# Running the DeltaNet chains of two heads step by step beside each other in a hybrid decoder kernel

## The chip, the core and the metric

The kernel runs on one core of one Trainium2 chip, in one launch. The metric is the device time of that launch in microseconds (us), lower is better. The engines in the texts are PE (TensorE, the matrix engine), PEld (its weight loads), DVE (VectorE), ACT (ScalarE), POOL (GpSimd) and SP (SyncE, which here issues the DMAs). `L110` means line 110 of the kernel before.

## The reference

The kernel is one inference step of a trunk of two layers: 2048 prompt tokens with 16 learned meta tokens ahead of them, and 8 sample tokens with caches and states of their own. The width is 1024, all in float32. Layer AB projects its normed input once and feeds two mixers: window attention (8 query heads, 2 key heads, window 128, a learned sink per head) and gated DeltaNet (4 heads of 128, a short causal convolution on q, k and v, and a recurrent state). Both are gated, put side by side and projected back. Layer C is a gated linear attention (GLA) with 4 heads. The DeltaNet of one head, cut to its core:

```python
a_mat = jnp.where(strict, jnp.einsum('bnhik,bnhjk->bnhij', kbeta, kc) * decay, 0.0) + jnp.eye(CHUNK)
rhs = jnp.concatenate([vc * bc[..., None], kbeta * jnp.exp(gc)[..., None]], axis=-1)
sol = lax.linalg.triangular_solve(a_mat, rhs, left_side=True, lower=True, unit_diagonal=True)
u, w = sol[..., :B_DV], sol[..., B_DV:]
...
def step(S, xs):
    u_c, w_c, qk_c, qd_c, kd_c, gl_c = xs
    v_new = u_c - jnp.einsum('bhck,bhkv->bhcv', w_c, S)
    o = jnp.einsum('bhck,bhkv->bhcv', qd_c, S) + jnp.einsum('bhij,bhjv->bhiv', qk_c, v_new)
    S = S * gl_c[..., None, None] + jnp.einsum('bhck,bhcv->bhkv', kd_c, v_new)
    return S, o
```

So each head needs, for every chunk of tokens, the inverse of a unit lower triangular matrix (it is the same for all the right-hand sides), and then a scan over the chunks that carries the state `S`. The heads don't depend on each other.

## The kernel before, in words

**Tiling.** The prompt is worked in four groups of 512 tokens; group 0 carries 24 tokens more (8 sample, 16 meta), and works its columns in two halves of 268. A group goes through layer AB and then layer C. The activations lie transposed (features on partitions, tokens along the free axis).

**Two kinds of products.** The large projections come from `proj`: one output tile of 128 features takes 8 feature blocks of 3 matmuls each (values are split into a high and a low part in a rounded float type, and high x high, high x low and low x high are added up), with 512 columns. They accumulate in the PSUM pool `pp`, 4 buffers. All the small products (DeltaNet, attention, GLA) are plain f32 matmuls and accumulate in the PSUM pool `pc`, also 4 buffers, which `cb` hands out. `MM` is the helper at L110, and `TT`, `STT` and `TS` are those at L113, L116 and L120, so most rows of the profile bear these lines; tiles tell them apart (`wh` and `wl` are the high and the low part of a weight).

**The planner.** The program's order is worked out in Python while the program is built. The projections are the trunk: `bulk` (L406) issues them and adds what three matmuls take to a clock of TensorE, `Clock.pe`. Everything else is a chain: a generator that emits a step and then yields two numbers, the time until its next step is due and what the step cost TensorE. `spawn` (L383) puts a chain into a lane; the chains of one lane run one after another. After every three projection matmuls `bulk` runs those chains whose step is due (`step`, L392). `join` (L418) runs chains until the named ones are done, without any projection between them. `take` and `give` (L434, L442) count work tiles: tag `T` has 52 slots with a cap of 47 (`NT - NT_FREE`), tag `BQ` has 4. Where there is no room, `take` runs the chains until there is; within a chain, `take_in` and `until` look again every 0.5 us of the planner's clock. The times until due are the table `LAT` (`DEF_LAT`, L34). The compiler's scheduler may still move an instruction within its engine's queue by the readiness that it models.

**The DeltaNet chain of a head**, `dn_head` (L1420), on four chunks of 128 tokens, with a yield between the steps:

1. four transposes of k (L1450), its norm on ACT, the decay (`R`), the products of k with k and q, four transposes of the masked product (`at`);
2. the inverse: first on DVE the 32x32 diagonal blocks (`i1`, L1498 to L1505), then four levels of doubling, each of two steps (`ia` and `ib`, L1506 to L1524) of 16 products of 32x32 with a DVE operation and a DVE transpose between them; then two steps of L1530 to L1551 that join blocks of 32 to 64, and two steps (L1554, L1559) of 64x64 products that join those to 128; the temporaries are the tiles `inv`, 6 buffers;
3. transposes of v and q (L1567, L1575), then for each chunk the three steps of the scan (`s1`, `s2`, `s3`, L1582 to L1602), then the norm, a last transpose and the gate.

The due times of a chain add up to 47.84 us. `ab_conv` takes 2 tiles of `T` (`CV` and the gate) and 2 of `BQ` (`CQ` and one that the chain works in) for a head, and its chain 7 more of `T` (2 in `chunks`, 5 in `dn_head`); of the 9, two stay until the output projection as the mixed tile.

**The order around the change.** `ab_conv` (L893) projects and convolves k, q and v of a head (j = 0, 1, 2), and spawns its chain into the lane "dn" at j = 1. In group 0 it also spawns the chains of the meta tokens (`meta`) and of the sample tokens (`dn_sample`), in lanes of their own. `ab_head` (L1044) does head 0; from group 1 on it runs within the previous group's `c_out` (L1303). `ab_rest` (L1050) follows the order

```python
ORDER = "c1 s0 c2 s1 c3 s2 s3".split()
```

where `c` is a DeltaNet head and `s` one of four pairs of attention heads: `ab_swa` (L957) takes 3 tiles, projects, and spawns `swa_pair` (L983), which takes 6 more and works four blocks of 128 queries (due times 21.7 us), in the lane "swa". Then `ab_out` (L1062) gives back the 16 tiles of the layer's input and projects the 8 mixed tiles to the output: a first half from those in `OUT_AB[:3]`, which are heads 0 and 1 and pair 0 (in group 0 heads 0 and 1 only), then a `join` of all DeltaNet and attention chains, then the second half. Layer C follows: `c_head` (L1239), `gla_head` (L1751), `c_out`.

Of the kernel before, what the change touches and what calls it, by code (L numbers as in the profile page):

```python
# [9 lines left out]
F32 = mybir.dt.float32  # L10
# [10 lines left out]
SMP = 8  # L21
META = 16
EX = SMP + META
NT, NT_FREE = 52, 5
NW = 8
AHEAD = 8
W_AHEAD = 1
RS_AT = 5

ORDER = "c1 s0 c2 s1 c3 s2 s3".split()  # L30

# [4 lines left out]
CMAX = EX + 512  # L36
# [33 lines left out]
def kernel(ctx: ExitStack, tc: tile.TileContext, ins, outs):  # L70
# [12 lines left out]
    def nm(s):  # L83
        cnt[0] += 1
        return f"{s}_{cnt[0]}"
# [9 lines left out]
        return ft(dt)  # L95

    def t512(shape=(128, 128), dt=F32):
        return wk.tile(list(shape), dt, tag="t512", bufs=4, name=nm("t5"))

    def sm(shape=(128, 32), dt=F32):  # L100
        return wk.tile(list(shape), dt, tag="sm", bufs=20, name=nm("sm"))

    def cb(shape=(128, 512)):
        return pc.tile(list(shape), F32, tag="pc", name=nm("pc"))
# [278 lines left out]
    def spawn(gen, lane, delay=1.0, tag=None):  # L383
        s = [Clock.pe + delay, gen, True, lane, tag]
        if lanes.setdefault(lane, []):
            lanes[lane].append(s)
        else:
            lanes[lane].append(s)
            streams.append(s)
        return s  # L390

    def step(s):  # L392
        try:
            lat, pe = next(s[1])
            s[0] += lat
            Clock.pe += pe
        except StopIteration:
            s[2] = False
            streams.remove(s)
            lanes[s[3]].pop(0)  # L400
            if lanes[s[3]]:
                n = lanes[s[3]][0]
                n[0] = max(n[0], s[0])
                streams.append(n)

    def bulk(gen, hooks=()):  # L406

        for i, c in enumerate(gen):
# [3 lines left out]
            while streams:  # L412
# [2 lines left out]
                    break  # L415
                step(s)

    def join(ss):  # L418
        while any(s[2] for s in ss):
            advance()  # L420


    live = {"BQ": 0, "T": 0}
    caps = {"BQ": 4, "T": NT - NT_FREE}

    def room(tag, n=1):
        return live[tag] + n <= caps[tag]
# [15 lines left out]
        live[tag] -= n  # L443

    def until(cond):
        while not cond():
            yield 0.5, 0.0

    def take_in(tag, n=1):
        yield from until(lambda: room(tag, n))  # L450
# [213 lines left out]
    def new_group(g):  # L664
        q = Grp()
        q.g = g
        q.C = CMAX if g == 0 else 512
        q.off = EX if g == 0 else 0
        q.halves = [(0, q.C // 2), (q.C // 2, q.C // 2)] if g == 0 else [(0, 512)]
        q.x0 = 0 if g == 0 else EX + 512 * g  # L670
        q.wins = [(b, q.off + 128 * b) for b in range(4)]
        q.seq0 = SMP if g == 0 else 0
        q.s0 = 1 if g == 0 else 0
        q.nscan = 4 + q.s0
        q.layer = "AB"
        q.M = [[None] * 8, [None] * 8]
        q.can_m = False
        q.dn = []
        q.sw = []
        return q  # L680

# [211 lines left out]
    def ab_conv(q, h):  # L893
        g = q.g
        take("BQ", 2)
        CQ = wk.tile([128, 2, CMAX - SMP], F32, tag="BQ", bufs=4, name=nm("CQ"))
        take("T", 2)
        CV = ft(shape=(128, CMAX - SMP))
        G_, vdone, done = [], [], []

        first, got = [], []

        def meta():
            yield from take_in("T")
            got.append(1)
            yield from dn_head(q, h, CQ, CV, 0, 1, 32, 0, G_, SMP, META, vdone, done, first)

        def chunks():
            if g == 0:
                yield from until(lambda: got)  # L910
            else:
                first.append(1)
            yield from take_in("T", 2)
            yield from dn_head(q, h, CQ, CV, META if g == 0 else 0, 4, 128, q.s0, G_, q.off, 128, vdone, done, first)
            give("BQ")
            give("T")
        for j in range(3):
            ct = 3 * h + j
            Tt = ft()

            def w(i):
                return PV[:, P_CW + 4 * ct + i:P_CW + 4 * ct + i + 1]

            def ev_c(ps, c0, n):

                m = n - q.seq0
                if g == 0:
                    A.copy(XS[:, ct, :], ps[:, 0:SMP])
                    R = ps[:, SMP - 3:n]
                    V.memset(R[:, 0:3], 0.0)  # L930
                else:
                    R = ft()
                    A.copy(R[:, 3:3 + m], ps)
                    G.tensor_copy(R[:, 0:3], hist[:, ct])
                A.activation(Tt[:, :m], R[:, 3:3 + m], AF.Copy, scale=w(3))
                for i in (2, 1, 0):
                    STT(Tt[:, :m], R[:, i:i + m], w(i), Tt[:, :m], mul, add)
                G.tensor_copy(hist[:, ct], R[:, m:m + 3])
                o = (CV if j == 2 else CQ[:, j])[:, :m]
                A.activation(o, Tt[:, :m], AF.Tanh, scale=0.5)  # L940
                STT(o, o, 1.0, Tt[:, :m], add, mul)
            bulk(ab_proj(q, 9 + ct, ev_c))
            if h == 0 and j == 0:
                bulk(ab_v(q))
            if j == 1:
                if g == 0:
                    q.dn.append(spawn(meta(), "dnx", 0.5, tag=h))
                s = spawn(chunks(), "dn", LAT["dn_spawn"], tag=h)
                q.dn.append(s)
        vdone.append(1)  # L950
        G_.append(ft())
        bulk(ab_proj(q, 21 + h, gate(q, G_[0], 4 + h)))
        done.append(1)
        if g == 0:
            q.dn.append(spawn(dn_sample(q, h), "smp", tag=h))
# [154 lines left out]
    def c_v(q, h):  # L1110
        g, s0 = q.g, q.s0
        take("BQ")
        VH = wk.tile([128, 4, 256], F32, tag="BQ", bufs=4, name=nm("VH"))
        if h == 0:
            gkp = cb()
            gkx = cb() if g == 0 else None

        def ev_vc(ps, slot):
            ex = slot == "e"
            rsc = q.rs[:, 4:5] if ex else q.rs[:, slot:slot + 1]  # L1120
            if ex:
                e = wk.tile([128, 256], F32, tag="SM", bufs=4, name=nm("exv"))
                A.activation(e[0:EX], ps[0:EX, 0:256], AF.Copy, scale=rsc[0:EX])
                q.VM = wk.tile([128, 256], F32, tag="SM", bufs=4, name=nm("vm"))
                SY.dma_start(q.VM[0:META], e[SMP:EX, :])
                q.VS = e
            else:
                A.activation(VH[:, slot, :], ps[:, 0:256], AF.Copy, scale=rsc)
            if h == 0:
                gt = sm((128, 16))  # L1130
                if ex:
                    TS(gt[0:EX], ps[0:EX, 256:272], rsc[0:EX])
                    T.transpose(gkx[0:16, 0:EX], gt[0:EX], ident[0:EX, 0:EX])
                else:
                    TS(gt, ps[:, 256:272], rsc)
                    T.transpose(gkp[0:16, 128 * slot:128 * slot + 128], gt, ident)
        ws = ([("e", 0, ev_vc)] if g == 0 else []) + [(b, c0, ev_vc) for b, c0 in q.wins]
        if h == 0:
            yield from proj_tok(q, ("cv", h), q.H, 272, ws)
            for (src, c0, n) in [(gkp, q.off, 512)] + ([(gkx, 0, EX)] if g == 0 else []):  # L1140
                V.tensor_copy(GS[0:16, c0:c0 + n], src[0:16, 0:n])
                TT(GS[32:48, c0:c0 + n], src[0:16, 0:n], GS[0:16, c0:c0 + n].bitcast(F32), sub)
                V.tensor_copy(GS[64:80, c0:c0 + n], src[0:16, 0:n])
        else:
            yield from proj_tok(q, ("cv", h), q.H, 256, ws)
        q.VH = VH

    def c_logs(q):
# [3 lines left out]
        yield from take_in("BQ", 2)  # L1152
        q.mn, Bs = [], []
        for p in range(2):
            B = wk.tile([128, 2, CMAX], F32, tag="BQ", bufs=4, name=nm("Bc"))
            for h in (2 * p, 2 * p + 1):
                mn = ft()
                bg = PV[:, P_BGK + h:P_BGK + h + 1]
# [80 lines left out]
    def c_head(q, h, nxt):  # L1239
# [8 lines left out]
        join([q.dec])  # L1248
        E = q.E
        take("BQ", 2)  # L1250
        QKt = wk.tile([128, 2, CMAX], F32, tag="BQ", bufs=4, name=nm("QKt"))
        for j in range(2):
            def ev_m(ps, c0, n):
                TT(QKt[:, j, c0:c0 + n], ps, E[j][:, c0:c0 + n], mul)
# [165 lines left out]
    def dn_head(q, h, CQ, CV, q0, nch, L, s0, G_, mc0, nv, vdone, done, first):  # L1420
# [47 lines left out]
            A.activation(DT[R_, c, 0:L], Rp[R_, c, 0:L], AF.Exp, bias=SC["ng"][R_, s0 + c, h:h + 1])  # L1468
        yield LAT["dn_R"], 0.45 * pe
        if L == 128:  # L1470
            BQ = wk.tile([128, 4, 2, 128], F32, tag="BQ", bufs=4, name=nm("BQ"))
        else:
            BQ = ftt((128, 1, 64)).rearrange("p c (x l) -> p c x l", x=2)
        for c0 in range(0, nch, 2):
# [18 lines left out]


        yield LAT["dn_at"], 0.45 * pe
        tc4 = lambda: wk.tile([128, 4, 32], F32, tag="inv", bufs=6, name=nm("inv"))

        P1, Y, X = tc4(), tc4(), tc4()  # L1498
        for a in range(nb):
# [60 lines left out]
            A.copy(YF[0:64, :, 64:128], pi[0:64, 1])  # L1560
            yield 0.0, 0.4

        while not vdone:
            yield 0.5, 0.0
        vT = cb((128, 4, 128))
        for c in range(nch):
            T.transpose(vT[R_, c], blk(2, c), ident)  # L1567
# [46 lines left out]
        on = O  # L1614
        TT(on[R_, 0:nch], O[R_, 0:nch], bc(st2[R_, 3, 0:nch], 128), mul)
        yield LAT["dn_n"], 0.0
        while not (done and q.can_m):
            yield 0.5, 0.0
        oT = cb((128, 4, 128))
        for c in range(nch):  # L1620
            T.transpose(oT[:, c, 0:L], on[R_, c], ident[R_, 0:L])
# [129 lines left out]
    def gla_head(qq, h, QKt, VH, ce, Gz, done):  # L1751
# [14 lines left out]
        A.copy(KT, kT)  # L1766
        yield LAT["gl_t"], 1.4
        st = sm((128, 4, 4))
        On = wk.tile([128, 4, 256], F32, tag="BQ", bufs=4, name=nm("On"))
        QS = ft(shape=(128, 4, 128))  # L1770
        TT(QS, QKt[:, 0, off:off + 512].rearrange("p (c t) -> p c t", c=4), bc(ce[:, s0:s0 + 4], 128), mul)
        for c0 in (0, 2):
# [31 lines left out]

    def gla_sample(q, h, QKt, VS, ea, Gz):
        vrow = rows_of(VS[0:8], 256)
        QZ = wk.tile([128, 72], F32, tag="t512", bufs=4, name=nm("QZ"))
        V.memset(QZ, 0.0)
        V.tensor_copy(QZ.rearrange("p (b x) -> p x b", x=9)[:, 0, :], QKt[:, 0, 0:SMP])
        o = cb()  # L1810
# [155 lines left out]
```

## Time and profile before

| what | value |
| --- | --- |
| time, median of 3 runs | 2223.04 us (2221.27 to 2227.0) |
| profiled execution, its own time | 2224.94 us |
| span of its trace | 2223.2 us |
| TensorE clock granted, mean | 0.986 of full speed |
| HBM over the span | 179 GB/s |
| DMA packets' time, share of 16 engines | 52.6% (queue of SP) |

The profile is of one execution. Its page lists the busy time of each engine, the chain of work that ended last, and the groups of instructions by line and tile. The busy time of one engine in the groups is a sum over instructions that overlap (matmuls are pipelined), so the distance from the start of one matmul to that of the next is what it costs TensorE's queue, and less than its duration. A row of a group reads: line, engine, operation, output tile <- input tiles, tile shape, number; then busy time and mean duration in ns; then the idle time ahead of these instructions and what ended most of it. A row of the timeline reads: start in us from the span's start, duration, engine, line, operation, tiles, shape, and the number of like instructions in a row; in brackets what it waited for. "x32" in a row of f32 products means 16 products, since an f32 matmul leaves two records.

### The profile page before, as it was taken

The numbers are of one execution on the slowest core, as the hardware profiler recorded it, in microseconds if no ns is written. First come the engines' busy times: TensorE is split into PE (matmuls) and PEld (weight loads), VectorE is DVE, ScalarE is ACT, GpSimd is POOL, SyncE is SP. The second block draws the span as 40 slices with busy tenths as digits, with TensorE's granted clock in tenths as the row PEclk, the third lists the DMA queues.
The fourth block names the chain that finished last, engine by engine and source line by source line (L and its number), as shares of the span: only waits on it lengthen the run. The fifth ranks groups of instructions, "written<-read, shape, count | busy, mean of one in ns | idle before, by whom it ended". The sixth has DMA issues, their size and how long they took to land.

```text
span 2223.2 us, 43787 instructions
## 1 busy us (share of the span) xinstructions
PE 2152.0 (97%) x17290; PEld 1809.8 (81%) x17290; DVE 1231.0 (55%) x3501; ACT 835.4 (38%) x2235; POOL 263.6 (12%) x314
## 2 busy tenths in 40 slices
PE   8889999999999999999999999999999999999997
PEld 8878888888879777788887777788887877778886
DVE  7768876655464566544344466545344466654323
ACT  5435444443352244333332244334333233334222
POOL 0011100021210011002220011002130000001111
PEclk9989999999999999999999999999999999999999
DMA  6643537767766723464555733365554743274444
GB/s 236 211 155 121 175 118 263 253 218 261 253 204 244 242 96 103 135 239 142 181 204 164 267 107 102 125 218 169 180 198 147 245 147 114 86 259 156 157 149 156
DMA packets 162622, 400.17 MB, mean 180 GB/s; under 512 B 22048, under 2 KB 54464, under 8 KB 162384
## 3 DMA queue, kind: packets, MB, share of 16 engines
q1 hardware_dynamic: 162416, 397.37, 52.6%
q8 instruction: 136, 2.23, 0.4%
q14 instruction: 70, 0.57, 0.1%
HBM read 297.19 MB, written 101.70 MB: 179 GB/s over the span
## 4 chain that ended last, share of the span: by engine, by line
PE 69%; DVE 5%; DMA 2%; ACT 2%; issue 2%; POOL 1%; SPq 0%; DVEq 0%; POOLq 0%; ACTq 0%
PE pp L110 53%; PE pc L110 14%; DVE t L116 2%; DVE t L113 1%; DVE inv L113 1%; PE pc L1015 1%; DMA t<-in_xT 1%; PE pc L1796 1%; DMA t<-x2d 1%; POOL sm L206 0%; DVE t L120 0%; DVE t L999 0%; PE pc L1575 0%; PE pc L1450 0%; DMA t<-rows 0%
## 5 line engine op out<-in xcount | busy, mean ns | idle before, releaser
L110 PE MATMUL pp<-t,wh 128*128 128x512 f32 (+1 forms) x4528 | 1265.8, 364 | 17.7 <-DVE t L113 7.7
L110 PEld LDWEIGHTS pp<-t,wh 128*128 128x128 f32 x4528 | 782.6, 191 | 128.4 <-issue 19.6
L110 PE MATMUL pp<-t,wl 128*128 128x512 f32 (+1 forms) x2264 | 808.8, 358 | 1.9 <-DVE wl L113 1.7
L110 PEld LDWEIGHTS pp<-t,wl 128*128 128x128 f32 x2264 | 429.8, 190 | 60.5 <-DVE wl L113 2.7
L113 POOL TENSOR_TENSOR t<-t,t 128x512 fp32r<-128x512 f32 (+3 forms) x128 | 163.8, 1298 | 517.3 <-ACT t L660 275.1
L110 PE MATMUL pp<-wh,t 128*128 128x256 f32 (+1 forms) x1088 | 209.0, 288 | 3.8 <-DVE QKt L113 3.8
L116 DVE SCALAR_TENSOR_TENSOR t<-t,PV,t 128x512 f32<-128x512 f32 (+4 forms) x232 | 176.0, 768 | 60.0 <-ACT t L1098 24.3
L110 PEld LDWEIGHTS pp<-wh,t 128*128 128x128 f32 x1088 | 172.4, 190 | 6.0 <-DVE QKt L113 4.0
L206 POOL TENSOR_TENSOR sm<-sm,mh 128x2 f32<-128x2 f32 (+3 forms) x84 | 68.4, 814 | 812.3 <-DVE sm L116 367.5
L116 DVE SCALAR_TENSOR_TENSOR t<-pp,t 128x512 f32<-128x512 f32 (+3 forms) x160 | 93.1, 586 | 120.0 <-PE pp L110 67.5
L110 PE MATMUL pp<-wl,t 128*128 128x256 f32 (+1 forms) x544 | 155.8, 286 | 0.0
L113 DVE TENSOR_TENSOR wl<-raw,wh 128x512 fp32r<-128x512 f32 (+3 forms) x138 | 92.2, 685 | 23.3 <-PE pp L110 10.9
L110 PEld LDWEIGHTS pp<-wl,t 128*128 128x128 f32 x544 | 103.4, 190 | 0.6
L365 ACT CAST wh<-raw 128x512 fp32r<-128x512 f32 (+2 forms) x122 | 68.0, 588 | 50.6 <-DMA raw<-in_w_c 17.0
L113 DVE TENSOR_TENSOR t<-t,t 128x512 f32<-128x512 f32 (+4 forms) x103 | 62.9, 614 | 41.3 <-ACT t L489 40.0
L113 DVE TENSOR_TENSOR QKt<-pp,t 128x512 f32<-128x512 f32 (+1 forms) x40 | 23.3, 586 | 111.0 <-PE pp L110 95.6
L110 PEld LDWEIGHTS pc<-t,t 128*128 128x128 f32 (+4 forms) x496 | 62.9, 162 | 22.2 <-DVE t L116 4.0
L489 ACT ACTIVATE t<-t 128x512 f32<-128x512 f32 (+1 forms) x70 | 44.1, 631 | 97.5 <-DVE t L116 69.0
L1004 ACT ACTIVATE t<-t,sm 128x257 f32<-128x257 f32 x128 | 64.2, 504 | 43.4 <-DVE sm L116 42.7
L110 PE MATMUL pc<-t,t 128*128 128x128 f32 (+5 forms) x496 | 78.1, 267 | 1.6 <-DVE t L116 0.8
L113 DVE TENSOR_TENSOR t<-pp,t 128x268 f32<-128x268 f32 (+1 forms) x90 | 44.4, 497 | 50.3 <-PE pp L110 36.0
L1017 ACT COPY t<-pc 128x512 f32<-128x512 f32 x64 | 37.5, 586 | 79.5 <-PE pc L1015 77.7
(334 smaller groups left out, 2806.5 us busy)
## 6 DMA issues: line engine op xcount, KB each, us to landing
wh<-wd SPq DMA_DIRECT2D x157, 512.0 KB, 3.6
wl<-wd SPq DMA_DIRECT2D x157, 512.0 KB, 4.5
wd<-wh SPq DMA_DIRECT2D x55, 512.0 KB, 4.0
wd<-wl SPq DMA_DIRECT2D x55, 512.0 KB, 5.6
t<-in_xT SPq DMA_DIRECT2D x72, 256.0 KB, 4.6
raw<-in_w_ab SPq DMA_DIRECT2D x25, 512.0 KB, 5.7
raw<-in_w_c SPq DMA_DIRECT2D x16, 512.0 KB, 4.9
out_yp<-t SPq DMA_DIRECT2D x32, 256.0 KB, 2.5
```

Of the source, the lines that this page charges most:

```text
L110: T.matmul(out, lhsT, rhs, start=start, stop=stop)
L113: return (eng or V).tensor_tensor(out, a, b, op=op)
L116: V.scalar_tensor_tensor(out, a, s, b, op0=op0, op1=op1)
L206: G.tensor_tensor(out, x, mh[0:x.shape[0]].to_broadcast(list(x.shape)), op=ALU.pow)
L365: last[0] = A.copy(hi[:, c], raw[:, c])
L489: A.activation(sq[:, :q.C], x, AF.Square)
L1004: A.activation(S_[:, kv], S_[:, kv], AF.Exp, bias=st[:, 2 + kv:3 + kv], accum_out=st[:, 4 + kv:5 + kv])
L1015: T.transpose(pt[:, kv, x], S_[:, kv, 128 * x:128 * x + 128], ident)
L1017: A.copy(PT, pt)
L1796: T.transpose(oT[:, c], On[:, c, 128 * j:128 * j + 128], ident)
```

## The change

A generator `together` takes the chains of two heads and runs them in lockstep: one step of each, then a single yield, whose due time is the longer of the two times 1.25 (`PAIR_LAT`) and whose cost is the sum. Where one of the two waits, it now yields `None`, and `together` passes the wait on and asks the same chain again, so the other head doesn't run ahead. `ab_conv` no longer spawns a chain at j = 1 of each head but collects it in `q.pair`, and spawns the pair at j = 1 of the odd head: heads 0 and 1, then heads 2 and 3, in the same lane. The chains of meta and sample tokens are spawned as before.

The two waits in `dn_head` that were loops of their own (for v, and for the gate) are now `until` too. For two chains at a time there are more temporaries: `BQ` 6 slots for 4 (and its cap), `t512` 8 for 4, `sm` 24 for 20, `inv` 10 for 6. The cap of `T` stays. To make room for these in SBUF the kernel is built with a smaller scratch for DMA descriptors (`dynamic_dma_scratch_size=1024`).

```diff
+NBQ = 6
+PAIR_LAT = 1.25
...
-        return wk.tile(list(shape), dt, tag="t512", bufs=4, name=nm("t5"))
+        return wk.tile(list(shape), dt, tag="t512", bufs=8, name=nm("t5"))
...
-        return wk.tile(list(shape), dt, tag="sm", bufs=20, name=nm("sm"))
+        return wk.tile(list(shape), dt, tag="sm", bufs=24, name=nm("sm"))
...
             lat, pe = next(s[1])
-            s[0] += lat
+            s[0] += 0.5 if lat is None else lat
...
+    def together(gens):
+
+        gens = list(gens)
+        while gens:
+            lat, pe = [], 0.0
+            for gen in list(gens):
+                r = next(gen, False)
+                while r and r[0] is None:
+                    yield r
+                    r = next(gen, False)
+                if r:
+                    lat.append(r[0])
+                    pe += r[1]
+                else:
+                    gens.remove(gen)
+            if lat:
+                yield max(lat) * PAIR_LAT if len(lat) > 1 else lat[0], pe
...
-    caps = {"BQ": 4, "T": NT - NT_FREE}
+    caps = {"BQ": NBQ, "T": NT - NT_FREE}
...
         while not cond():
-            yield 0.5, 0.0
+            yield None, 0.0
...
+        q.pair = []
...
-                s = spawn(chunks(), "dn", LAT["dn_spawn"], tag=h)
-                q.dn.append(s)
+                q.pair.append(chunks())
+                if h % 2:
+                    q.dn.append(spawn(together(q.pair), "dn", LAT["dn_spawn"], tag=h))
+                    q.pair = []
...
-        tc4 = lambda: wk.tile([128, 4, 32], F32, tag="inv", bufs=6, name=nm("inv"))
+        tc4 = lambda: wk.tile([128, 4, 32], F32, tag="inv", bufs=10, name=nm("inv"))
...
-        while not vdone:
-            yield 0.5, 0.0
+        yield from until(lambda: vdone)
...
-        while not (done and q.can_m):
-            yield 0.5, 0.0
+        yield from until(lambda: done and q.can_m)
...
-    nc = _bacc.Bacc("TRN2", target_bir_lowering=False, num_devices=1)
+    nc = _bacc.Bacc("TRN2", target_bir_lowering=False, num_devices=1, dynamic_dma_scratch_size=1024)
```

The other lines of the diff put `NBQ` in place of 4, and 8 in place of 4 for one more `t512` tile.

More of the change, by code (lines that the diff above doesn't have):

```diff
@@ L895, in ab_conv @@
         take("BQ", 2)
-        CQ = wk.tile([128, 2, CMAX - SMP], F32, tag="BQ", bufs=4, name=nm("CQ"))
+        CQ = wk.tile([128, 2, CMAX - SMP], F32, tag="BQ", bufs=NBQ, name=nm("CQ"))
         take("T", 2)
@@ L1112, in c_v @@
         take("BQ")
-        VH = wk.tile([128, 4, 256], F32, tag="BQ", bufs=4, name=nm("VH"))
+        VH = wk.tile([128, 4, 256], F32, tag="BQ", bufs=NBQ, name=nm("VH"))
         if h == 0:
@@ L1154, in c_logs @@
         for p in range(2):
-            B = wk.tile([128, 2, CMAX], F32, tag="BQ", bufs=4, name=nm("Bc"))
+            B = wk.tile([128, 2, CMAX], F32, tag="BQ", bufs=NBQ, name=nm("Bc"))
             for h in (2 * p, 2 * p + 1):
@@ L1250, in c_head @@
         take("BQ", 2)
-        QKt = wk.tile([128, 2, CMAX], F32, tag="BQ", bufs=4, name=nm("QKt"))
+        QKt = wk.tile([128, 2, CMAX], F32, tag="BQ", bufs=NBQ, name=nm("QKt"))
         for j in range(2):
@@ L1470, in dn_head @@
         if L == 128:
-            BQ = wk.tile([128, 4, 2, 128], F32, tag="BQ", bufs=4, name=nm("BQ"))
+            BQ = wk.tile([128, 4, 2, 128], F32, tag="BQ", bufs=NBQ, name=nm("BQ"))
         else:
@@ L1768, in gla_head @@
         st = sm((128, 4, 4))
-        On = wk.tile([128, 4, 256], F32, tag="BQ", bufs=4, name=nm("On"))
+        On = wk.tile([128, 4, 256], F32, tag="BQ", bufs=NBQ, name=nm("On"))
         QS = ft(shape=(128, 4, 128))
@@ L1806, in gla_sample @@
         vrow = rows_of(VS[0:8], 256)
-        QZ = wk.tile([128, 72], F32, tag="t512", bufs=4, name=nm("QZ"))
+        QZ = wk.tile([128, 72], F32, tag="t512", bufs=8, name=nm("QZ"))
         V.memset(QZ, 0.0)
```

## The prediction

> **What bounds the kernel now.** I read the page first (busy times, chain), then the groups of instructions, then PE's timeline around the small products. The page and its chain of waits:
>
> ```profile
> span 2223.2 us, 43787 instructions
> PE 2152.0 (97%) x17290; PEld 1809.8 (81%) x17290; DVE 1231.0 (55%) x3501; ACT 835.4 (38%) x2235; POOL 263.6 (12%) x314
> ...
> PE 69%; DVE 5%; DMA 2%; ACT 2%; issue 2%; POOL 1%; SPq 0%; DVEq 0%; POOLq 0%; ACTq 0%
> PE pp L110 53%; PE pc L110 14%; DVE t L116 2%; DVE t L113 1%; DVE inv L113 1%; PE pc L1015 1%; DMA t<-in_xT 1%; PE pc L1796 1%; DMA t<-x2d 1%; POOL sm L206 0%; DVE t L120 0%; DVE t L999 0%; PE pc L1575 0%; PE pc L1450 0%; DMA t<-rows 0%
> ```
>
> TensorE is the bound: it carries the chain, and the large projections (`pp`) and the small products (`pc`) queue on it one behind the other. So the change is worth what it takes from PE's queue, less what it leaves PE waiting for. The small products of the DeltaNet inverse are these two groups:
>
> ```profile
> L110 PE MATMUL pc<-inv,inv 32*32 32x32 f32 x2456 | 44.0, 197 | 1.4 <-DVE inv L113 1.4
> ...
> L110 PE MATMUL pc<-inv,t 32*32 32x32 f32 x2328 | 39.8, 197 | 12.6 <-DVE inv L113 12.1 <-issue 0.2
> ```
>
> Their busy time is 84 us, but busy time is not their price. PE's timeline in the second group, in start order (start, duration, ...; the row of the two `wh` matmuls between is left out):
>
> ```profile
> 880.19 0.40 PE L110 MATMUL pp<-t,wl 128*128 128x512 f32 x1
> 880.52 0.45 PE L110 MATMUL pc<-inv,inv 32*32 32x32 f32 x32
> ...
> 881.47 0.40 PE L110 MATMUL pp<-t,wl 128*128 128x512 f32 x1
> ...
> 882.73 0.39 PE L110 MATMUL pp<-t,wl 128*128 128x512 f32 x1
> ...
> 883.42 0.40 PE L110 MATMUL pp<-t,wl 128*128 128x512 f32 x1
> ```
>
> Undisturbed, three projection matmuls go by in 883.42 - 882.73 = 0.69 us (0.23 each). With one step of the inverse among them it is 881.47 - 880.19 = 1.28, so a step costs 0.59. Its 32 records (16 f32 products, two passes each) start within 0.45 - 0.197 = 0.25 us. The other **0.34 us is the way into and out of the 32x32 form**: the last wide matmul must run out, and the first one after cannot be loaded ahead. This is paid per step, whatever the step holds.
>
> **The change, part by part.**
>
> *Two heads in one step.* A chain has ten 32x32 steps (two per level for four levels, and two of L1537 to L1551): 160 in 16 chains. Side by side they are 80, so up to 80 x 0.34 = 27.2 us go. In two of the ten, the first of the inverse and the second `dn_m1` step, the second head's operand is late (below), and I count these merges as lost: 64 x 0.34 = 21.8. The two 64x64 steps of a chain (L1554, L1559) merge 16 times; no row has one alone between projections, so each saves between 0 and 0.34, and I take the middle, 2.7, because it is the same kind of change of form with longer products. Together **-24.5**, with ends 0 (no two heads stay adjacent) and -32.6 (96 x 0.34). In the Trainium skill, TensorEngine Tiling (Array Packing), Key Properties, it says that changing the tiling mode drains TensorE; by that rule the 64x64 steps would save the full 0.34 too, and the sum would be 2.7 us lower.
>
> Steps of full-size products gain nothing by company:
>
> ```profile
> 909.75 0.39 PE L110 MATMUL pp<-t,wl 128*128 128x512 f32 x1
> 909.99 0.60 PE L1015 MATMUL pc<-CC,t 128*128 128x128 f32 x4
> ...
> 910.89 0.40 PE L110 MATMUL pp<-t,wl 128*128 128x512 f32 x1
> ...
> 923.42 0.40 PE L110 MATMUL pp<-t,wl 128*128 128x512 f32 x1
> 923.66 0.63 PE L110 MATMUL pc<-kh,t 128*128 128x256 f32 x4
> ...
> 924.60 0.39 PE L110 MATMUL pp<-t,wl 128*128 128x512 f32 x1
> ...
> 928.10 0.39 PE L110 MATMUL pp<-t,wl 128*128 128x512 f32 x1
> 928.33 0.64 PE L110 MATMUL pc<-kh,t 128*128 128x256 f32 x4
> 928.81 0.60 PE L1015 MATMUL pc<-CC,t 128*128 128x128 f32 x4
> ...
> 929.70 0.40 PE L110 MATMUL pp<-t,wl 128*128 128x512 f32 x1
> ```
>
> Alone these cost 1.14 - 0.69 = 0.45 and 1.18 - 0.69 = 0.49, together 1.60 - 0.69 = 0.91. That is 0.03 less than the sum, so the rest of a chain (transposes, scan) counts 0.
>
> *Waits of PE on a step's inputs.* The waits of PE from 654 us on (us in total, times, longest):
>
> ```profile
> PE pc L110 <- DVE inv L113: 8.6, 9, 1.8
> PE pc L1450 <- DVE CQ L116: 4.5, 6, 1.2
> ```
>
> The second row is a chain's first transposes waiting for its `CQ`. In a pair the even head's come first and have long been ready, which covers half: **-2** (0 to -4). The first row is the first step of the inverse. Vector work ahead of it and of the second `dn_m1` step:
>
> ```profile
> 867.38 1.16 DVE L113 TENSOR_TENSOR inv<-t,CC 32x128 f32<-32x128 f32 x4
> 868.58 0.31 DVE L1502 STREAM_TRANSPOSE inv<-inv 128x128 f32<-128x128 f32 x1
> ...
> 881.61 1.39 DVE L113 TENSOR_TENSOR t<-inv,CC 128x128 f32<-128x128 f32 x8
> 883.01 0.59 DVE L120 TENSOR_SCALAR inv<-pc 32x128 f32<-32x128 f32 x2
> ```
>
> With two subtractions of some 0.25 the first is 1.95 us per head, the second 1.98, and DVE does head after head. The factor 1.25 on due times gives 0.35 + 0.45 = 0.8 and 0.33 + 0.48 = 0.8 more. So the second head is about 1.15 and 1.2 us late. If PE stood still for it, that is 8 x 2.35 = 18.8. I expect the compile-time order to put projections there instead (the windows below show that it moves them): then only the merge is lost, as counted, and **+4** for what the order misjudges, as in the 8.6 us of today (0 to +18.8). Between the other steps DVE has about 0.6 us per head; a pair's step and the bulk until the next one take more than that twice over.
>
> *The even head starts later.* Head 0 no longer runs from the second convolution of its own head on. In groups 1 to 3 this only moves it from under the output projection to under others. In group 0 it stood alone:
>
> ```profile
> 53.17 0.28 PE L110 MATMUL pp<-t,wl 128*128 128x268 f32 x1
> ...
> 68.17 1.26 PE L110 MATMUL pp<-t,wh 128*128 128x268 f32 x4
> ...
> 56.98 1.16 ACT L365 CAST wh<-raw 128x512 fp32r<-128x512 f32 x2
> ...
> 861.04 0.63 PE L1450 MATMUL pc<-CC,CQ 128*128 128x128 f32 x4 [1.22 <-DVE CQ L116]
> ...
> 861.97 1.03 PE L110 MATMUL pc<-CQ 128*128 128x256 f32 x4
> 862.93 0.66 PE L110 MATMUL pc<-t,va 128*64 128x128 f32 x8
> ```
>
> For 68.17 - 53.17 = 15 us there is no projection, only the chain up to its eighth 32x32 step. Among projections the same costs 8 x 0.59 = 4.7, plus 0.93 (861.04 to 861.97) for transposes and decay, 2 x 0.96 for k and q, some 0.4 for the next transposes: 8 us. So 7 us go if the weights are there; their cast, behind the chain on ACT, ended at 58.14, 5 us into the gap. I take **-3** (+8 if the projection still starts at 68.17, -7 if at once).
>
> *Tiles.* The cap of work tiles stays 47. When `s2` and `s3` have been projected, 16 inputs, 4 of heads 0 and 1, 4 of `s0` and `s1`, 16 of the running pair and 3 + 3 of `s2`, `s3` are live: 46. `swa_pair` of `s2` wants 6 more and waits; with one chain running it was 40 + 6 = 46 and it started. Now it starts when `ab_out` returns 16, after `s3`, and two window-attention chains of 21.7 us by their due times lie behind each other there, 43 us. What covered the one chain until now:
>
> ```profile
> 912.70:945.20 32.50, 32.10 (x189) 24.23 (x187) 18.23 (x68) 11.19 (x31) 3.88 (x3) 1.00 0.63 202
> ...
> 912.70:945.20 32.50, 25.48 (x97) 16.56 (x95) 6.21 (x9) 0.54 (x1) 1.00 0.63 202
> ...
> 945.20 0.50 PE L110 MATMUL pp<-t,wh 128*128 128x512 f32 x1 [0.38 <-POOL t L113]
> ```
>
> The first row is all work in the window, the second the `pp` tiles alone: 97 projection matmuls, though `ab_out`'s first half has 8 x 9 = 72, so some 25 of the second half were pulled ahead, and PE was busy 32.1 of 32.5 us. The first half is 72 x 0.23 = 16.5 us; four `pp` buffers let at most 48 come ahead, 11 us; the attention's own products, 8 blocks of 0.45 + 0.49 + 0.7 (the eight `va` products, by the row of 862.93), are 13. That is 40.5 against 43: I take **+2** a group, +6 for groups 1 to 3 (0 to 7.8 each, the rival below). Group 0 starts with one more input tile and has sample chains of 5 tiles each, so `take` of `s2` and `s3` itself blocks until the pair lets go: by due times some 20 us, in which PE still has the moved head's products and what can be pulled ahead. **+5** (0 to 20).
>
> *Buffers.* More slots for `t512`, `sm`, `inv` and `BQ` cost PE nothing; the smaller DMA scratch makes the room, and SP's queue alone issues (the page's queues). Four `pc` banks now serve two chains and the window attention; no row shows that pressure, so by the nearest (8.6 us of waits) between 0 and +8: **+2**.
>
> Sum: -24.5 - 2 + 4 - 3 + 6 + 5 + 2 = **-12.5**. The profiled execution took 2224.94 (span 2223.2), 1.9 above the median of the runs, 2223.04. So 2212.4 in its own terms, 2210.5 for a median; I say **2211**.
>
> **The rivals.**
>
> *Slower: the attention tail.* Place: end of the AB layer of each group. If no more than today's 25 matmuls can be pulled ahead, the cover is 16.5 + 5.7 + 13 = 35.2 of 43, and 7.8 us a group are bare. With 10 instead of 5 in group 0: -24.5 - 2 + 4 - 3 + 31 + 10 + 2 = +17.5, about 2240. It decides from 4.6 us a group on, where four tails eat the 18.5 that the other terms leave. For it: the 25, and the wait of 0.38 at the end. Against: PE was full, so more than 25 was never asked for.
>
> *No change: DVE bounds the step.* PE stands for the second head, 18.8 instead of 4: +2.3, 2225. For it: the 8.6 us of waits in today's first step. Against: nine waits only, and none at `dn_m1`. The Trainium skill, TensorEngine Tiling (Array Packing), PSUM Bottleneck, warns that packing speeds TensorE up but not the evacuation of PSUM; by that rule this case would weigh more than I give it.
>
> *The change doesn't do what it says.* The compile-time order goes by modelled readiness and parts the two heads; a quarter of the merges remain: -6 instead of -24.5, +6, 2229.
>
> *All of it.* 96 merges hold, and tails and tiles cost nothing: -32.6 - 2 + 4 - 3 + 2, 2191.
>
> **How the numbers follow.** Forecast 0.45 (2200 to 2221), tail 0.20, DVE 0.15, parted heads 0.08, all of it 0.12. About 0.3%, 6.7 us, can be told from no change. Faster: all of the last, most of the first, a little of DVE, 0.52; same 0.25; slower 0.23, nearly all the tail. The range takes in the best case and the tail, 2190 to 2241.
>
> **What would show it.** PE rows of `pc<-inv` with x64 where x32 stood, and 1.1 us instead of two times 0.59 for them. The wait of PE on `inv` near 8.6 us; 25 or more says DVE. In the windows from the last gate of a group to the first row of `ab_out`'s second half: more than 97 `pp` matmuls and PE full, or PE idle and the tail decides. From 53 us on in group 0, projections by 58. Wrong would make me: rows of x32 with projections between (parted heads), or PE waits on a `pc` bank.

## The result, and the profile after

The changed kernel took 2284.11 us (median of 4 runs, 2278.72 to 2290.33) against 2222.26 for the kernel before: the ratio is 1.0278, with a 95% interval of 1.0252 to 1.0303. It is 62 us slower; 2211, faster, was forecast. The profiled execution took 2290.33 us. Its page begins:

```profile
span 2288.3 us, 43794 instructions
PE 2187.1 (96%) x17290; PEld 1851.3 (81%) x17290; DVE 1220.6 (53%) x3501; ACT 834.2 (36%) x2235; POOL 265.7 (12%) x314
...
PE 67%; DVE 4%; DMA 3%; issue 3%; ACT 2%; POOL 1%; SPq 0%; DVEq 0%; ACTq 0%; POOLq 0%
```

There are as many PE records as before, and less DVE work. Yet PE was busy 35 us longer and stood 30 us longer. The view of the cores gives the first hint (span, granted clock); before, the clock was 0.986:

```profile
core 0: 2288.3 us, clock 0.958
```

And the waits of PE in the changed kernel (us in total, times, longest) give the second:

```profile
PE pc L112 <- issue: 27.7, 20, 4.0
PE pp L112 <- DMA wl<-wd: 8.6, 3, 2.9
...
PE pc L112 <- DVE inv L115: 6.4, 14, 2.0
PE pc L1039 <- DVE t L122: 6.1, 9, 0.9
...
PE pc L1474 <- DVE CQ L118: 3.0, 4, 1.6
```

"issue" means that PE waited for nothing that the profile shows. Before it was one such wait:

```profile
PE pc L110 <- issue: 0.2, 1, 0.2
```

PE's timeline in the inverse of heads 0 and 1 of group 1 shows where they lie (start, duration):

```profile
769.57 0.50 PE L112 MATMUL pp<-t,wh 128*128 128x512 f32 x1
769.90 0.39 PE L112 MATMUL pp<-t,wl 128*128 128x512 f32 x1
770.13 0.39 PE L112 MATMUL pp<-t,wh 128*128 128x512 f32 x1
770.45 0.45 PE L112 MATMUL pc<-inv,t 32*32 32x32 f32 x32
770.73 0.43 PE L112 MATMUL pc<-inv,inv 32*32 32x32 f32 x27
774.05 0.75 PE L112 MATMUL pc<-inv,inv 32*32 32x32 f32 x37 [2.90 <-issue]
774.76 0.65 PE L112 MATMUL pc<-inv,t 32*32 32x32 f32 x32
775.34 0.80 PE L112 MATMUL pp<-t,wh 128*128 128x512 f32 x1
776.07 0.65 PE L112 MATMUL pc<-inv,t 32*32 32x32 f32 x32
776.52 0.61 PE L112 MATMUL pc<-inv,inv 32*32 32x32 f32 x26
777.78 0.75 PE L112 MATMUL pc<-inv,inv 32*32 32x32 f32 x38 [0.65 <-issue]
```

The two heads are side by side as meant. But in the middle of one step, after 27 of 64 records, PE stops for 2.9 us, and for 0.65 us in a later one. Behind the first stop every record is longer: a projection matmul 0.80 where it was 0.50. The windows of this stretch (busy time of each engine, then granted clock, DMA share, GB/s):

```profile
764.50:771.20 6.70, 6.66 (x234) 4.48 (x233) 4.94 (x15) 1.59 (x3) 0.00 (x0) 1.00 0.97 338
771.20:774.10 2.90, 0.05 (x5) 0.05 (x7) 0.07 (x1) 0.00 (x0) 0.00 (x0) 0.91 0.33 130
774.10:787.30 13.20, 11.85 (x336) 8.96 (x336) 8.41 (x37) 0.00 (x0) 0.00 (x0) 0.50 0.02 4
```

For 13 us behind the stop the clock is at half. From 620 us on, that is in groups 1 to 3, the records of the clock hold 108 us at half, before 12. The count of DMA packets by queue from 770.4 to 784.5 us says what came meanwhile:

```profile
q1 hardware_dynamic: 193, 0.67, 12.0%
q8 instruction: 4, 0.07, 1.9%
```

On the whole page queue 8 has 136 packets and 2.23 MB, 16 KB each. PE and PEld have 17290 records each, 34580 in all, so 2.23 MB are 64 bytes for one. **Queue 8 brings PE its instructions, 256 in a packet** (the bursts below confirm it), and a step of two heads is 64 records on PE and 64 on PEld, 128 instructions. The theory that the experiments test: PE ran out of instructions.

### The profile page after: what moved, and what is told of

Its sections match the earlier page's. It is cut to its first block, busy times and chain, and to the rows that moved or that the text cites. A ratio compares the mean times of both kernels' runs of the same rounds, so it can differ in the third digit from the quotient of the medians.

```text
span 2288.3 us, 43794 instructions
## 1 busy us (share of the span) xinstructions
PE 2187.1 (96%) x17290; PEld 1851.3 (81%) x17290; DVE 1220.6 (53%) x3501; ACT 834.2 (36%) x2235; POOL 265.7 (12%) x314
## 3 DMA queue, kind: packets, MB, share of 16 engines
q8 instruction: 136, 2.23, 0.4%
## 4 chain that ended last, share of the span: by engine, by line
PE 67%; DVE 4%; DMA 3%; issue 3%; ACT 2%; POOL 1%; SPq 0%; DVEq 0%; ACTq 0%; POOLq 0%
PE pp L112 51%; PE pc L112 13%; DMA t<-x1d 1%; DVE t L115 1%; DVE t L118 1%; PE pc L1039 1%; POOL sm L208 1%; DMA wl<-wd 1%; DVE inv L115 1%; PE pc L1818 1%; ACT junk L1476 0%; DVE BQ L115 0%; PE pc L1590 0%; DMA t<-rows 0%; PE pc L1786 0%
## 5 line engine op out<-in xcount | busy, mean ns | idle before, releaser
L112 PEld LDWEIGHTS pp<-t,wh 128*128 128x128 f32 x4528 | 799.4, 193 | 130.3 <-issue 14.0
L112 PEld LDWEIGHTS pp<-t,wl 128*128 128x128 f32 x2264 | 436.5, 193 | 71.6 <-DMA wl<-wd 9.9
L208 POOL TENSOR_TENSOR sm<-sm,mh 128x4 f32<-128x4 f32 (+3 forms) x84 | 67.9, 808 | 712.7 <-DVE sm L118 299.2
L112 PEld LDWEIGHTS pc<-inv,t 32*32 32x32 f32 x2328 | 37.2, 122 | 44.3 <-issue 28.2
```

Source lines behind the costliest of these rows:

```text
L112: T.matmul(out, lhsT, rhs, start=start, stop=stop)
L208: G.tensor_tensor(out, x, mh[0:x.shape[0]].to_broadcast(list(x.shape)), op=ALU.pow)
```

## The experiments

Each ran beside runs of the kernel before on the same chip (medians 2219.3 to 2219.9). Times are medians of 4 to 12 runs; e4 and e8 are one run each. A name such as e5 stands for the label that begins so.

**The buffers alone** (e1). The kernel before with

```diff
-    nc = _bacc.Bacc("TRN2", target_bir_lowering=False, num_devices=1)
+    nc = _bacc.Bacc("TRN2", target_bir_lowering=False, num_devices=1, dynamic_dma_scratch_size=1024)
```

and the change's slot numbers for `BQ`, `t512`, `sm` and `inv`.

> The kernel before, with the change's larger buffers and its smaller DMA scratch, and no pairing. Every theory in which the pairing is the cause: the time of before, 2222 us within 0.3%, granted clock 0.986. If the buffers or the scratch were part of the loss, up to 2284.

2219.39 us, ratio 0.9996 (0.9977 to 1.0016). Buffers and scratch cost nothing by themselves, so the loss comes with the pairing.

**The inverse one head after the other** (e2). The yields from `dn_at` to `dn_m2` carry a mark, and `together` runs a marked stretch of one head to its end:

```diff
-                while r and r[0] is None:
+                while r and (r[0] is None or len(r) > 2):
```

> The changed kernel, but the steps of the inverse (from i1 to the second 64x64 product) run for one head of a pair and then for the other, each step at its own due time; all else stays paired, with the same starts and tiles. Theory of supply (PE runs out of instructions in a step with two heads' 32x32 products, and the clock falls to half behind the gap): issue waits of PE from 27.7 us to under 6, clock from 0.958 to 0.98 or more, time 2225 to 2245. Rival (late starts, tiles and the attention tail cost the time): these are as late or later here, so 2275 or more. Rival (PE waits for the second head's vector work): waits on inv fall, the clock stays near 0.958, 2265 to 2280.

2257.30 us, ratio 1.0168 (1.0130 to 1.0206); issue waits 0.5 us, clock 0.981. 27 us of the 62 go, and with them all issue waits. The time is 12 us above what was expected of supply: something else costs too, and the merges are lost here. Its trace is 28 us behind that of the kernel before, and 20 of them are there by the 3000th of 8792 projection matmuls, near the end of group 0, so most of the rest is group 0's.

**The inverse in lockstep, with more space** (e3). A marked step's due time is stretched by 2.5 instead of 1.25:

```diff
+INV_LAT = 2.5
...
-                yield max(lat) * PAIR_LAT if len(lat) > 1 else lat[0], pe
+                yield max(lat) * (INV_LAT if inv else PAIR_LAT) if len(lat) > 1 else lat[0], pe
```

> The changed kernel with the inverse still in lockstep, but its steps spaced at 2.5 times the single head's due time instead of 1.25. Theory of supply: what counts is instructions per time, so two steps (256 instructions) in 6.5 us no longer outrun packets that come every 3.5 us: issue waits under 6 us, clock 0.98 or more, and the merged steps still save, 2200 to 2235. Rival (late starts and tail): each pair ends some 20 us later, so slower than the changed kernel, 2290 or more. Rival (two heads in a step are slow by themselves): 2275 to 2290.

2242.65 us, ratio 1.0106 (1.0067 to 1.0144); issue waits 7.3 us (under 6 were expected), clock 0.980. **One constant, which lengthens the chains, gives back 41 us** (39 by the times of the kernel before that ran beside each). So it isn't two heads in a step, nor late starts, but how many such steps come in a time. 8 us above the range of supply remain. This trace is 14 us behind that of the kernel before at the 3000th projection matmul and at the last one: what is left is group 0's.

**Bursts that measure the supply and the clock** (e4). After layer AB of groups 1 and 2 of the kernel before stand products that nothing uses:

```diff
+            MM(ps.rearrange("p a (b k) -> p (a b) k", b=4)[r, c], x[r, 0:32].bitcast(F32), x[r, 32 * c:32 * c + 32].bitcast(F32))
...
+                MM(ps[0:32, 0:512], x[0:32, 0:32].bitcast(F32), x[0:32, 0:512].bitcast(F32))
...
+        if g == 1:
+            burst(q.H[0][7], 512)
+        if g == 2:
+            thin(q.H[0][7], 24)
```

> The kernel before with two bursts of products that nothing uses, behind the AB layer: in group 1, 512 products of 32x32 (2048 instructions, eight packets of 16 KB); in group 2, 24 products of 32x32 by 512 columns (96 instructions, a sixteenth of the array). Theory of supply: the first burst takes 20 to 29 us, in stretches of 256 instructions with gaps in which PE waits for nothing shown, one packet of the instruction queue in each, 3.4 us or more apart; by the records' spacing of 8.2 ns alone it would be 8.4 us without gaps. For the clock: if gaps of PE bring it to half, it is half in the first burst and full in the second; if low use of the array does, it is half in the second too.

PE's timeline of the first burst, and behind it the second:

```profile
967.67 1.99 PE L110 MATMUL pc<-t 32*32 32x32 f32 x213
974.99 1.93 PE L110 MATMUL pc<-t 32*32 32x32 f32 x128 [5.34 <-issue]
978.46 1.93 PE L110 MATMUL pc<-t 32*32 32x32 f32 x128 [1.55 <-issue]
981.93 1.93 PE L110 MATMUL pc<-t 32*32 32x32 f32 x128 [1.54 <-issue]
...
996.37 0.85 PE L110 MATMUL pc<-t 32*32 32x32 f32 x43 [1.82 <-issue]
...
1509.96 36.04 PE L110 MATMUL pc<-t 32*32 32x512 f32 x48
```

The burst takes 29.5 us, just above the expected 20 to 29, and it comes in portions of 128 records, 256 instructions: one packet each. 978.46 - 974.99 = **3.47 us for a packet** (later ones up to 3.75), of which 1.54 are a gap; the first gap is 5.34. The traffic is light in the later portions (66 GB/s over the burst, mostly at its start), so there it is no lack of bandwidth. The longer first gap began in heavy traffic (347 GB/s in the 7.6 us up to the burst); whether that lengthened it wasn't tried. The windows of the second burst:

```profile
1509.90:1515.20 5.30, 5.30 (x14) 1.35 (x14) 1.35 (x2) 0.52 (x2) 0.00 (x0) 1.00 0.89 331
1515.20:1545.90 30.70, 30.70 (x37) 5.93 (x35) 0.00 (x0) 0.00 (x0) 0.00 (x0) 0.50 0.01 3
```

PE is busy without a gap, yet from 5.3 us on its clock is half. So on the clock the alternative holds: work on 32 of the array's 128 rows and columns is enough to lose it. A gap isn't needed; the first burst alone couldn't have shown that. It is one stretch of one run.

**Group 0 with single heads** (e5), groups 1 to 3 paired:

```diff
-                if h % 2:
+                if h % 2 or g == 0:
```

> The changed kernel with the heads of group 0 one after another as before, and pairs in groups 1 to 3 only. At the end of layer AB of group 0 the changed kernel's projections were some 25 us behind those of before, and 20 us behind at the end of its layer C. Theory (group 0's part is its own: moved head, blocked tiles, a bare tail): that part goes, about 20 us less, 2260 to 2268. Rival (the lag of group 0 is supply and clock as elsewhere and is half made up in any case): 2272 to 2284.

2261.53 us, ratio 1.0206 (1.0167 to 1.0246): 22.6 us less than the change. Part of this is supply again: the issue waits fell from 27.7 to 20.2 us. The 14 us of the spaced kernel suggest that group 0 also has a loss of its own.

**Both** (e6): the spaced inverse, and group 0 single.

> The kernel with the spaced inverse (2242.7 us) and group 0's heads one after another. Groups 1 to 3 took as long there as before, and its lag of 14 to 17 us was group 0's. If the two parts add up: 2222 to 2230, no different from before. If group 0's part is needed by what follows it: 2235 or more.

2226.95 us, ratio 1.0035 (1.0016 to 1.0054). Spacing took 41.5 us off (2284.1 to 2242.7), and single heads in group 0 another 15.7 (2242.7 to 2227.0), in the range that was expected if the parts add up. Unspaced, group 0 was worth 22.6, so some 7 us count in both. What is left is 7.6 us above the kernel before, although the merged steps save.

**Four tiles in the output's first half** (e7), on top of both:

```diff
-N_OUT0, N_OUT = 2, 3
+N_OUT0, N_OUT = 2, 4
```

> As the kernel before this one, with four instead of three of the eight mixed tiles in the first half of the output projection of groups 1 to 3, so 96 instead of 72 matmuls lie over the attention's last chains and fewer of the second half are pulled ahead. Theory of the tail (PE stands 2 to 3 us for the fifth pair of weights behind what was pulled ahead, and its clock is half for 3.4 us after it): those waits go, 5 us less a group, 2205 to 2215. Rival (the tail was covered, and the loss lies in the attention's own small products): the same as the kernel before this one within 5 us.

2224.28 us, ratio 1.0007 (0.9990 to 1.0024), 2.7 less, which is within the noise. PE's waits for `wl` went from 5.7 to 3.8 us, but the expected 5 us a group didn't come. The tail was mostly covered, as the rival had it; that the loss lies in the attention's own products is not shown by that.

**Every 32x32 product twice** (e8), in the kernel before: each `MM(pi[...])` of `ia`, `ib` and the two joining steps stands on two lines.

> The kernel before, no pairing, with every 32x32 product of the inverse and of the two joining steps issued twice into the same place: 64 more instructions per step, as many as a pair's step has, but one head, the same starts and tiles. By the records' spacing alone a step takes 0.25 us more, 0.25 x 160 = 40 us: 2260. Theory of supply: two steps (256 instructions and some of the projections) are due in about 3.1 us, less than the 3.5 us of a packet, so PE shows waits that end with nothing shown, 20 us or more, and a clock of 0.97 or less: 2290 or more.

2353.39 us, 134 more. PE's timeline:

```profile
699.66 0.85 PE L110 MATMUL pc<-inv,inv 32*32 32x32 f32 x64
700.43 0.39 PE L110 MATMUL pp<-t,wh 128*128 128x268 f32 x1
700.66 0.29 PE L110 MATMUL pp<-t,wl 128*128 128x268 f32 x1
700.79 0.41 PE L110 MATMUL pp<-t,wh 128*128 128x268 f32 x2
701.13 0.47 PE L110 MATMUL pc<-inv,t 32*32 32x32 f32 x29
702.32 0.53 PE L110 MATMUL pc<-inv,t 32*32 32x32 f32 x35 [0.71 <-issue]
```

A step takes 0.40 us more (0.85 instead of 0.45), not 0.25, which is at most 64 of the 134 us (160 x 0.40; some joining steps hold fewer products). Waits with nothing shown are 38.3 us in all (35.3 and 3.0); the rest, 32 us or more, wasn't traced to a cause. The clock is 0.974, where 0.97 or less was expected. So the same stops come without pairing, without moved starts, and with the tiles of before: it is the number of instructions in a time.

Traffic is not needed for a stop: ahead of the one shown (698.5 to 701.6 us) the DMA engines were busy 28% of the time. But the longest stop of this run, 3.20 us, came with them 96% busy (1340.0 to 1343.7 us), and ahead of the stop of 2.90 us in the changed kernel they were 97% busy. Whether traffic makes a stop longer wasn't tried.

**The first step later** (e9), on top of e7: the first step of a pair's inverse is due after 1.8 x 4.5 us.

```diff
+I1_LAT = 4.5
...
-        yield LAT["dn_i1"], 0.0, 1
+        yield LAT["dn_i1"], 0.0, I1_LAT
```

> As the kernel with the spaced inverse, group 0 single and four tiles in the first half (2224.3 us), with the first step of a pair's inverse due after 8.1 us instead of 4.5. There the second head's first products came about 3 us behind the first head's and ran into its next steps, and PE ran dry right behind them: its 9.3 us of waits with nothing shown lay in four such places. Theory of supply: those waits fall under 3 us and the half clock behind them goes, 2208 to 2216. Rival (merged steps save little, whatever the order): 2220 to 2228.

2217.82 us, ratio 0.9995 (0.9977 to 1.0013). Issue waits 4.4 us, where under 3 were expected, clock 0.986. The time lies 2 us above the range of supply and 2 below the rival's, and cannot be told from the kernel before.

**More space** (e10): `INV_LAT` 3.5 on top of e9.

> The same with the other steps of the inverse at 3.5 instead of 2.5 times. Theory of supply: at 2.5 packets are already slower to be used than to come, so more space gives nothing, and a pair's chain is some 15 us longer: within 5 us of the kernel before this one. If the supply still bound at 2.5: 5 us or more faster.

2227.29 us, ratio 1.0031 (1.0016 to 1.0046): 9.5 us slower than e9. Neither expectation came. More space isn't free: issue waits are 6.8 us, and the clock stands at half for 24 us from 1379 us on, in an inverse. Why the steps are denser there with more space wasn't tried.

## Why the prediction was wrong, point by point

**The step that failed: that an inverse step's further products cost only the spacing of their records.** "Its 32 records ... start within 0.45 - 0.197 = 0.25 us. The other 0.34 us is the way into and out of the 32x32 form." That is true of each step by itself, and the sum took a merged step to be free of all else. But with the due times times 1.25, two merged steps are due within 2 x 1.26 x 1.25 = 3.15 us, and their 256 instructions are a packet that takes 3.47. Before, two steps had 128 instructions in 2.5 us. The sum had no term for this, and neither had a rival: PE's instruction queue stood on the page (136 packets of 16 KB), and was read only to see that nothing else issues DMAs.

In the Trainium skill, Runtime: NRT & Kernel Launch, Instruction fetch mechanics, instructions are refilled in blocks of 16 KiB, 256 of them, while the sequencer works on the ones before; it calls the cost of crossing from one block to the next "mostly hidden". The block agrees with the 128 records of a portion here. That it is hidden doesn't hold for products of 32x32: the gap was 1.54 us of 3.47.

**The clock.** The prediction read 0.986 and took it as given. In groups 1 to 3 of the changed kernel six inverses have stops, and in each of them half clock begins within 3 us of a stop; in all it stands for 108 us there instead of 12. A projection matmul then takes 0.43 us in PE's queue and not 0.23 (986.39 to 987.67 for three in the row of the tail below). How the loss divides between the stops themselves and the half clock wasn't separated: the runs that removed most of the one removed most of the other. The stops are 27.5 us more than before; 96 us more at half clock are an estimated 48 us at most, if all the work there took twice its time. The nearest to a separation are e9 and e10: 2.4 us more of issue waits, some 29 us more at half clock in groups 1 to 3, and 9.5 us more time. The Trainium skill, TensorE: Matmul & The Clock Gate, Part 1, says that the gate follows how busy PE has been, in windows of about 3.4 us. The stretches at half in the changed kernel are multiples of 3.41 us (13.65 behind the stop shown; the one that runs on past the last instruction aside), which agrees; but a PE without a gap for 30 us was at half too (e4), so "busy" must be more than having an instruction.

**The merges: the saving of one is a little smaller, the count was luck.** Stretches of 32x32 products without a projection between them fell from 174 to 110, 64 fewer as counted ("64 x 0.34"). But not as meant: only 10 of them hold a pair's 64 records, and 21 hold 96 or more, several steps back to back. The spaced kernel (e3) has 60 fewer than before, and 41 of its stretches hold 64. A merged step in its timeline:

```profile
1908.66 0.40 PE L113 MATMUL pp<-t,wl 128*128 128x512 f32 x1
1908.98 0.75 PE L113 MATMUL pc<-inv,t 32*32 32x32 f32 x64
1909.67 0.73 PE L113 MATMUL pp<-t,wh 128*128 128x512 f32 x2
1910.24 0.39 PE L113 MATMUL pp<-t,wl 128*128 128x512 f32 x1
```

From 1908.66 to 1910.24 are three projection matmuls and the step, 1.58 us, so the step costs 1.58 - 0.69 = 0.89 against two times 0.59: it saves 0.29, and 64 would save some 19 us for 21.8. No kernel here shows this in its time: none with merged steps was faster than the kernel before, and what takes the saving up wasn't found. The 1.1 us that the last part gave for it was a slip; by its own terms it was 0.84.

**Waits on inputs: one term right, one not needed.** `CQ` fell from 4.5 to 3.0 (forecast -2). Waits on `inv` fell from 13.4 over the whole run to 6.4, where the sum had +4; a PE that is late for other reasons also waits less for them. Vector work is not the bound; that rival falls. New are the 6.1 us in which the attention's transposes wait for their operands (L1039; 0.4 before), which the sum didn't have.

**The moved head and the blocked tiles of group 0: 20 us instead of 2.** This is a second place where the sum failed. The gain at the start came: projections go on at 61.2 us instead of 68.2.

```profile
61.24 1.04 PE L112 MATMUL pp<-t,wh 128*128 128x268 f32 x3
```

But the layer as a whole lost. Two windows of group 0, of `pp` tiles alone, first of the kernel before and then of the changed one; the second ends at the first row of the output's second half:

```profile
53.20:248.80 195.60, 117.34 (x731) 99.01 (x730) 13.06 (x31) 0.00 (x0) 0.94 0.49 163
248.80:360.50 111.70, 67.31 (x426) 56.83 (x425) 12.94 (x31) 0.00 (x0) 0.97 0.47 150
```

```profile
53.20:248.80 195.60, 122.99 (x794) 107.92 (x792) 13.46 (x32) 0.00 (x0) 0.92 0.53 177
248.80:384.00 135.20, 61.35 (x367) 51.30 (x368) 12.46 (x30) 0.00 (x0) 0.87 0.32 101
```

At 248.8 us the changed kernel is some 60 projection matmuls ahead. It does not simply keep the gain of the start: counted from 53.2 us on it leads by 78 at 100 us (246 against 168) and is 18 behind at 200 us (521 against 539), with the stops of its first pair between. And the lead is given back: these are the matmuls that lay over the chains later. For the rest of the layer it has 59 fewer, the chains stand bare, the clock is 0.87, and the stretch takes 23.5 us longer. Single heads there (e5) took 22.6 us off. How much of it is the moved start, the tiles or the supply wasn't tried; stops of 2.29 and 0.23 us and 24 us at half clock (from 282 us on) lie in that stretch, so some is supply.

**The attention tail: the cover came, and something else was late.** The join comes later, and more of the second half is pulled ahead. Two windows from behind the last DeltaNet transposes to PE's stop, of all work and of `pp` tiles alone:

```profile
940.60:982.30 41.70, 41.27 (x246) 31.32 (x244) 22.18 (x88) 16.50 (x44) 5.13 (x4) 1.00 0.49 153
...
940.60:982.30 41.70, 31.98 (x119) 20.95 (x119) 6.21 (x9) 0.00 (x0) 1.00 0.49 153
```

PE is full, with 119 projection matmuls. So the cap of four `pp` buffers, 48 matmuls, is what was nearly reached (119 - 72 = 47, if the window holds only the first half and what was pulled ahead). Then something else is late, the fifth pair of weights:

```profile
981.59 0.63 PE L112 MATMUL pp<-t,wh 128*128 128x512 f32 x2
985.07 0.67 PE L112 MATMUL pp<-t,wl 128*128 128x512 f32 x1 [2.85 <-DMA wl<-wd]
985.54 1.05 PE L112 MATMUL pp<-t,wh 128*128 128x512 f32 x2
986.39 0.63 PE L112 MATMUL pp<-t,wl 128*128 128x512 f32 x1
986.82 1.05 PE L112 MATMUL pp<-t,wh 128*128 128x512 f32 x2
987.67 0.63 PE L112 MATMUL pp<-t,wl 128*128 128x512 f32 x1
```

The timeline of SP's queue has the loads:

```profile
960.63 0.56 SPq L265 DMA_DIRECT2D wl<-wd  x1
978.30 0.32 SPq L265 DMA_DIRECT2D wh<-wd  x1
```

For 17.7 us there is none: SP waits for PE there (17.3 us in one wait), since the eight weight tiles (`NW`) are held by what was pulled ahead. That is 2.9 us a group and 3.4 us at half clock behind it, at most 1.7 more: above the +2 of the forecast, and below the 7.8 of the rival that gave 2240. That rival had the sign of the result, but not its cause.

**The parted heads** came in part: 34 stretches of a single head's 32 records are left (114 before), and the spaced kernel (e3) has 15. It is no main cause: e2, which parts nearly all of them, is 27 us faster than the changed kernel.

## What to carry to other kernels

Count instructions in a time, not only time in an engine: when small products are made denser, compare their number with the packets of the engine's instruction queue on the page, and look in the waits for "issue" and at the granted clock right behind it. Work that is packed closer together on an engine that has to be filled from outside can be slower than the same work spread among long instructions; one spacing constant was worth 41 us of 62 here. And work moved to a later place takes its cover with it only if the cover moves too: what group 0 gained at its start was missing at its end.

## What the hardware showed that was not expected

- PE's instructions came in packets of 256 that in a dense run of 32x32 products were 3.47 to 3.75 us apart, with DMA nearly idle; the first stop was 5.34 us in the burst, and in the changed kernel stops reached 2.90 (with DMA 97% busy ahead of it) and 4.0.
- 32x32 products on 512 columns, without a gap between them, had the granted clock at half from 5.3 us on, for 30.7 us.
- 16 products issued a second time into the same places of PSUM cost 0.40 us, where 16 products more into other places cost 0.30 (rows of 64 records took 0.85 in e8 and 0.75 in e3, those of 32 took 0.45).
